# Hybrid decoder block: two operand kinds of the first output projection split into pairs early, second-half convolution outputs stored whole, T2 stored whole, one step between a fetch and its use

## The chip, the cores and the metric

One core of one Trainium2 chip runs the whole block. The metric is device time in microseconds (us); lower is better. The kernel before was timed in three runs; a profile of one further execution gives the trace that is read here. TensorE is called PE, its weight loads PEld, VectorE DVE, ScalarE ACT, GpSimd POOL, and SyncE SP; SP issues nearly all DMAs.

## The reference, cut to what matters

```python
h = rmsnorm(x, norm1_g)                                    # x: 2048 positions x 1024
p_q, p_k, p_v, p_g, p_a, c_b, c_c, c_h = split(h @ w_in)   # one input projection
o_gla = rmsnorm(gla_chunked(q, k, v, log_a), gla_norm_g) * silu(p_g)   # 4 heads x 128
o_conv = c_b * causal_depthwise_conv(c_c * c_h, conv_w)    # 512 wide, width 3
x = x + concat([o_gla, o_conv]) @ w_out                    # the output projection
h2 = rmsnorm(x, norm2_g)
x = x + (silu(h2 @ w_ffn_gate) * (h2 @ w_ffn_up)) @ w_ffn_down
return rmsnorm(x, norm_f_g)
```

Everything is float32. `gla_chunked` is gated linear attention with a state carried along the positions, so it runs in order.

## The kernel before, in words

**Layout.** Features lie on the 128 partitions and positions on the free axis, in four blocks of 512. The first *half* is blocks 0 and 1, the second half blocks 2 and 3.

**Pairs.** A float32 operand is multiplied as a pair: `split` (L206, L207) makes `hi` on ACT (a rounded copy) and `lo` on DVE (the rest). One product of two pairs is three 128x512 matmuls in a row: `wh*xh` (L503), `wh*xl` (L504) and `wl*xh` (L505), which are nearly all of PE's work.

**Units.** `unit` computes a 2x2 block of output tiles by seven products instead of eight (`PRODUCTS`: A11*B11, S1*T1, S2*T2, A12*B21, S3*T3, S4*B22, A22*T4). A, S are weight quarters and their sums, made and split inside the unit; B, T are activation operands, four tiles of 128x512 of each kind. A product takes 12 matmuls in most units, so a unit is 84. Between products an ACT copy (`copied`, L549) or a DVE addition (`plus`, L537) takes a PSUM bank's content out; the next product that accumulates into that bank waits for it. `weights_in_step` (with `after=`) makes the weights of a unit product by product, bound to the unit's own progress; `unit_weights` makes them as soon as the scheduler finds room.

**Operands from memory.** An operand kind is stored to DRAM either as a finished pair (twice the bytes, `load_pair` brings both parts) or whole (`load_undivided`), and then it is split on ACT and DVE where `due(n)` calls for it in the first unit, or at once (`load_whole`). `WHOLE` names the kinds T3, B22 and T4 that are stored whole.

**Order of the program.** (1) `opening`; (2) `in_proj(0)`, the units of the first half; (3) `in_proj(1)`, twelve units on the second half, here called second-half units 0 to 11: two for k and q, two for v, two for the gate, and twice three (cc, ch, cb) for the convolution; (4) `out_proj_in_sevens`, four units of the first half's output projection, here out-projection units 0 to 3; (5) `out_proj`, the plain output projection of the second half; (6) the feed-forward layer, both halves. Beside the units runs a list of *background* steps (`tick`, called after each product, takes steps from it; most run at every second product): `h1_ahead` makes the operands of the second half, `gate` the forget gate, `gla_half(0)` and `gla_half(1)` the attention chunks (16 in all), `mix_differences` the differences of the mixed outputs. `gla_half` fetches a chunk with 14 small DMAs, takes an exponential of the decay `ee` on ACT (L1173, L1174), multiplies (L1175, L1176), and then PE makes scores, transposes and outputs. All chunks and units take their PSUM banks from one pool of eight.

**Places that matter here.** In (3), the multiplication by c_b (L1121) finishes convolution outputs; in the second half each is split at once (eight splits, `hi<-c` on ACT and `c<-c,hi` on DVE) and stored as a pair. At the end of (3), `mix_operands` loads the operands of (4); B11 and T1 come whole and all eight of their tiles are split in one go, the kinds behind them at their `due` points. A scheduler sets the order of each engine's instructions when the program is built; `behind(marks)` and `issue_after` tell it what an instruction has to stand behind. Each engine then works its queue off in that order.

In the trace, second-half unit 0 lies at 259 to 284 us, unit 2 at 307 to 336, unit 9 at 483 to 514, unit 11 at 542 to 568; out-projection unit 0 at 568 to 603, unit 3 at 650 to 674.

Of the kernel before, what the change touches and what calls it, by code (L numbers as in the profile page):

```python
# [46 lines left out]
WHOLE = ("T3", "B22", "T4")  # L47

# [6 lines left out]
def tile_hymba_block(ctx, tc, x, xt, win, wa, wgu, wout, wffn, wdown, wdown_first, small, out):  # L55
# [54 lines left out]
    def made_ahead(name, n):  # L110
        return dram.tile([P, PB] if n in WHOLE else [P, 2, PB], F32, name=name)

# [3 lines left out]
    s_mix = [  # L116
        [dram.tile([P] + parts[b] + [PB], F32, name=f"sm{b}_{k}") for k in range(4)]
        for b in range(NB)
    ]
# [21 lines left out]
        n: [made_ahead(f"sh{n}_{k}", n) for k in range(4)] for _, n in PRODUCTS  # L141
    }
    s_h1 = {
        n: [made_ahead(f"si{n}_{k}", n) for k in range(4)] for _, n in PRODUCTS
# [129 lines left out]
    pace, ahead, hurry, steady, hasty = [0], [], [], [], []  # L274
# [232 lines left out]
    def unit(src, ops, into=None, onto=None, raw=None, between=(), rest=None, after=None, midway=None):  # L507
# [46 lines left out]
        c11 = copied("c11", oa, (0, 0))  # L554
        next(flow, None)
# [428 lines left out]
    def load_pairs(src):  # L984
        ops = no_operands()
        for _, n in PRODUCTS:
            ops[n] = [(load_undivided if n in WHOLE else load_pair)(p) for p in src[n]]
            if n in WHOLE:
                undivided[n] = ops[n]
        return ops  # L990
# [90 lines left out]
    def in_proj(half, ops, raw=None, between=(), rest=None):  # L1081
        def units():
            if half == 0:
                yield unit(win[2], ops, raw=raw, between=between, rest=rest)
            for u in range(0 if half else 3, 12):
                yield unit(win[u], ops, after=2 if half and u < 3 else None)
# [12 lines left out]
        for i0 in (0, 2):  # L1099
# [19 lines left out]
            for r, j, c, _ in next(units):  # L1119
                y = made[r, j] = cc[r, j]  # L1120
                dve.tensor_tensor(y[:], c[:], y[:], ALU.mult)  # L1121
                if half == 0:
                    store(s_mix[j][i0 + r][:], y[:])
                    if (r, 1 - j) in made:
                        t1 = tt("t1")
                        dve.tensor_tensor(t1[:], made[r, 1][:], made[r, 0][:], ALU.subtract)
                        store(s_diff["T1"][i0 + r][:], t1[:])
                    continue
                hi = tp.tile([P, PB], F32R, name="hi", tag="t")
                split(y[:], hi[:], y[:].bitcast(F32R))  # L1130
                dst = s_mix[2 * half + j][i0 + r]
                store(dst[:, 0, :], hi[:].bitcast(F32))
                store(dst[:, 1, :], y[:])


    def gla_half(half):
# [4 lines left out]
        yield  # L1141
        with tc.issue_after(tables.ins):
# [186 lines left out]

    def mix_operands():  # L1330
        src = {"B11": [y[:] for y in s_mix[0]], "B21": [s_gla[0][:, k] for k in range(4)]}
        src.update({"B22": [s_gla[1][:, k] for k in range(4)], **s_diff})
# [137 lines left out]
    def h2_ahead(ssq):  # L1470
# [8 lines left out]
        def put(n, k, h):  # L1479
            if n in WHOLE:  # L1480
# [6 lines left out]
    def load_h2():  # L1487
        ops, loads = no_operands(), raw_loads[-2]
        for _, n in PRODUCTS:
            for k in range(4):  # L1490
                with tc.issue_after(loads.ins):
                    o = (load_whole if n in WHOLE else load_pair)(s_h2p[n][k])
# [308 lines left out]
    ops = load_pairs(s_h1)  # L1801
    background.extend(
# [123 lines left out]
```

## Time and profile before

| | us |
|---|---|
| median of 3 runs (lowest, highest) | 2045.01 (2043.81, 2049.0) |
| the profiled execution's own time | 2044.2 |
| its span, first to last instruction | 2042.4 |
| PE busy in the span | 2010.8 |
| DVE busy | 1574.5 |
| ACT busy | 981.9 |

The span is 1.8 us shorter than the profiled execution's own time: what lies around it is small. In windows, the columns are window, length, then busy time and (count) of PE, PEld, DVE, ACT and POOL, the granted share of the PE clock (PEclk), the mean busy share of the 16 DMA engines, and GB/s. In a list of waits, a row is the waiting engine, its tile and line, what ended the wait, and then total us, times, longest us. In a timeline, a row is start, length, engine, line, operation, out<-in, and in brackets the idle time before it and what ended it; equal neighbours are one row with a count.

### The profile page before, as it was taken

The numbers are of one execution on the slowest core, as the hardware profiler recorded it, in microseconds if no ns is written. First come the engines' busy times: TensorE is split into PE (matmuls) and PEld (weight loads), VectorE is DVE, ScalarE is ACT, GpSimd is POOL, SyncE is SP. The second block draws the span as 40 slices with busy tenths as digits, with TensorE's granted clock in tenths as the row PEclk, the third lists the DMA queues.
The fourth block names the chain that finished last, engine by engine and source line by source line (L and its number), as shares of the span: only waits on it lengthen the run. The fifth ranks groups of instructions, "written<-read, shape, count | busy, mean of one in ns | idle before, by whom it ended". The sixth has DMA issues, their size and how long they took to land.

```text
span 2042.4 us, 27016 instructions
## 1 busy us (share of the span) xinstructions
PE 2010.8 (98%) x9251; PEld 1652.8 (81%) x9251; DVE 1574.5 (77%) x2831; ACT 981.9 (48%) x1941; POOL 10.3 (1%) x17
## 2 busy tenths in 40 slices
PE   9999999998989999999999999999999999999998
PEld 8888877787868888888888888887888888888886
DVE  7878868558887787778777688887777767778886
ACT  6664455654654344444444452334434444454345
POOL 0000000000000000000000000000000000000001
PEclk9999999999989999999999999999999999999998
DMA  7356865437687973446445576577444444486653
GB/s 263 128 202 219 285 260 176 135 122 266 194 277 246 346 269 134 170 171 219 164 159 196 192 292 242 188 283 292 157 168 170 158 147 170 175 331 221 247 216 129
DMA packets 192426, 427.78 MB, mean 209 GB/s; under 512 B 20544, under 2 KB 63776, under 8 KB 182816
## 3 DMA queue, kind: packets, MB, share of 16 engines
q1 hardware_dynamic: 191568, 425.40, 58.5%
q8 instruction: 73, 1.20, 0.2%
q10 hardware_dynamic: 720, 0.66, 0.1%
q14 instruction: 65, 0.53, 0.1%
HBM read 280.22 MB, written 145.75 MB: 209 GB/s over the span
## 4 chain that ended last, share of the span: by engine, by line
PE 94%; DVE 2%; ACT 2%; DMA 1%; issue 0%; SPq 0%; POOL 0%; POOLq 0%; DVEq 0%; ACTq 0%
PE mm L503 28%; PE mm L505 27%; PE mm L504 27%; PE mm L1394 1%; PE mm L1391 1%; PE mm L1392 1%; PE a_ps L1030 1%; PE mm L811 1%; PE mm L813 1%; PE mm L812 1%; PE o_ps L1211 1%; PE mm L1711 1%; DMA op<-sdT 1%; DVE wq L207 0%; PE o_ps L1218 0%
## 5 line engine op out<-in xcount | busy, mean ns | idle before, releaser
L503 PE MATMUL mm<-op,wq 128*128 128x512 f32 x2555 | 997.7, 393 | 9.2 <-ACT c L549 6.5
L504 PE MATMUL mm<-op,wq 128*128 128x512 f32 x2555 | 995.3, 390 | 0.0
L505 PE MATMUL mm<-op,wq 128*128 128x512 f32 x2555 | 985.9, 391 | 3.2 <-DVE wq L207 3.0
L206 ACT ACTIVATE wq<-raw 128x512 fp32r<-128x512 f32 (+2 forms) x620 | 362.1, 588 | 594.7 <-PE mm L505 500.3
L503 PEld LDWEIGHTS mm<-op,wq 128*128 128x128 f32 x2555 | 480.8, 188 | 115.9 <-ACT c L549 8.1
L505 PEld LDWEIGHTS mm<-op,wq 128*128 128x128 f32 x2555 | 480.7, 188 | 105.8 <-DVE wq L207 5.2
L504 PEld LDWEIGHTS mm<-op,wq 128*128 128x128 f32 x2555 | 481.1, 188 | 99.6 <-DVE op L207 1.5
L207 DVE TENSOR_TENSOR wq<-raw,wq 128x512 fp32r<-128x512 f32 (+2 forms) x620 | 390.9, 635 | 148.5 <-ACT wq L206 146.7
L537 DVE TENSOR_TENSOR y<-mm,y 128x512 f32<-128x512 f32 x213 | 145.6, 687 | 68.8 <-PE mm L505 67.9
L537 DVE TENSOR_TENSOR c<-mm,c 128x512 f32<-128x512 f32 x196 | 134.6, 687 | 74.3 <-PE mm L505 69.4
L549 ACT ACTIVATE c<-mm 128x512 f32<-128x512 f32 x198 | 115.3, 588 | 31.6 <-PE mm L505 28.4
L455 DVE TENSOR_TENSOR raw<-raw 128x512 f32<-128x512 f32 (+2 forms) x190 | 118.7, 631 | 2.2
L206 ACT ACTIVATE wq<-s 128x512 fp32r<-128x512 f32 (+2 forms) x100 | 58.9, 589 | 111.9 <-PE mm L505 98.5
L455 DVE TENSOR_TENSOR s<-raw 128x512 f32<-128x512 f32 (+2 forms) x95 | 60.0, 631 | 29.0 <-DMA raw<-in_wffn_dram 17.2
L207 DVE TENSOR_TENSOR op<-op 128x512 fp32r<-128x512 f32 x118 | 77.5, 682 | 3.7 <-ACT op L206 3.6
L206 ACT ACTIVATE op<-op 128x512 fp32r<-128x512 f32 x118 | 68.2, 621 | 11.4 <-DMA op<-sgla 5.2
L207 DVE TENSOR_TENSOR wq<-s,wq 128x512 fp32r<-128x512 f32 (+2 forms) x100 | 63.4, 634 | 2.1 <-ACT wq L206 1.3
L455 DVE TENSOR_TENSOR raw<-s,raw 128x512 f32<-128x512 f32 (+2 forms) x95 | 60.1, 633 | 1.4
L607 ACT ACTIVATE sg<-mm 128x512 f32<-128x512 f32 x26 | 15.5, 598 | 87.4 <-PE mm L505 87.3
L607 ACT ACTIVATE c<-c 128x512 f32<-128x512 f32 x78 | 48.9, 629 | 13.1 <-DVE c L537 10.5
L1392 PE MATMUL mm<-op,wq 128*128 128x512 f32 x128 | 50.2, 392 | 0.0
L1391 PE MATMUL mm<-op,wq 128*128 128x512 f32 x128 | 49.8, 389 | 0.0
(234 smaller groups left out, 1546.3 us busy)
## 6 DMA issues: line engine op xcount, KB each, us to landing
raw<-in_wffn_dram SPq DMA_DIRECT2D x44, 1024.0 KB, 6.2
sa_B<-so SPq DMA_DIRECT2D x47, 512.0 KB, 3.6
op<-sa_B SPq DMA_DIRECT2D x47, 512.0 KB, 6.5
raw<-in_win_dram SPq DMA_DIRECT2D x22, 1024.0 KB, 5.7
sa_T<-so SPq DMA_DIRECT2D x44, 512.0 KB, 4.4
op<-sa_T SPq DMA_DIRECT2D x44, 512.0 KB, 6.9
raw<-in_wdown_dram SPq DMA_DIRECT2D x24, 768.0 KB, 5.5
sx<-y SPq DMA_DIRECT2D x48, 256.0 KB, 4.1
```

What stands on the lines that cost most here:

```text
L206: last_hi[:] = [act.activation(hi, src, AF.Copy)]
L207: last_lo[:] = [dve.tensor_tensor(lo, src, hi.bitcast(F32), ALU.subtract)]
L455: dve.tensor_tensor(*args)
L503: pe.matmul(o[:], wh, xh, start=first and k == 0, stop=False, skip_group_check=True)
L504: pe.matmul(o[:], wh, xl, start=False, stop=False, skip_group_check=True)
L505: return pe.matmul(o[:], wl, xh, start=False, stop=k == n - 1, skip_group_check=True)
L537: last_plus[:] = [dve.tensor_tensor(t[:], o[:], t[:], ALU.add)]
L549: last_out[:] = [act.activation(t[:], o[:], AF.Copy)]
L607: last_silu[:] = [act.activation(s[:], c[:], AF.Silu)]
L811: pe.matmul(acc[:], wq[:, 0, c], p[:, 0, :], start=first, stop=False)
L1391: pe.matmul(o[e, j][:], wh, m[:, 0, :], start=n == 0, stop=False)
L1392: pe.matmul(o[e, j][:], wh, m[:, 1, :], start=False, stop=False)
```

## The change

- A list `MOSTLY` adds **T2** to the kinds stored whole, for the second half's input operands (`s_h1`) and the feed-forward operands made ahead (`s_h2p`). T2's splits move: for the input projection to a new `due("T2")` after the first product of second-half unit 0, for the feed-forward layer to its loading.
- **Early pairs.** A new generator `early_pairs` loads the eight tiles of B11 and T1 of the first output projection one by one, splits each and stores it as a pair (`s_pair`); `tick` takes one of its steps at every fourth product when nothing more urgent is due, and `mix_operands` runs what is left. Then `mix_operands` loads B11 and T1 with `load_pair`.
- **Convolution outputs** of the second half are stored whole. `build_mix` loads them with `load_whole`, which splits them there, marked to stand behind the fourth last `plus`.
- **Second-half unit 2** has its weights made by `unit_weights` instead of in step (`u < 2` for `u < 3`).
- `gla_half(1)` gets one more step between its first fetch and the first exponential.

```diff
+MOSTLY = ("T2", "T3", "B22", "T4")
...
-    s_mix = [
-        [dram.tile([P] + parts[b] + [PB], F32, name=f"sm{b}_{k}") for k in range(4)]
-        for b in range(NB)
-    ]
+    s_mix = scratch("sm", 4)
+    s_pair = {
+        n: [dram.tile([P, 2, PB], F32, name=f"sp{n}_{k}") for k in range(4)] for n in ("B11", "T1")
+    }
...
         elif hasty and pace[0] % 4 == 3:
             step()
+        elif pairs and pace[0] % 4 == 1:
+            next(pairs[0], None)
         elif ahead and pace[0] % 4 == 1:
             next(ahead[0], None)
...
         c11 = copied("c11", oa, (0, 0))
+        due("T2")
         next(flow, None)
...
     def h1_ahead():
         def put(n, k, h):
-            if n in WHOLE:
+            if n in MOSTLY:
                 store(s_h1[n][k][:], h[:])
...
-                yield unit(win[u], ops, after=2 if half and u < 3 else None)
+                yield unit(win[u], ops, after=2 if half and u < 2 else None)
...
-                if half == 0:
-                    store(s_mix[j][i0 + r][:], y[:])
...
-                hi = tp.tile([P, PB], F32R, name="hi", tag="t")
-                split(y[:], hi[:], y[:].bitcast(F32R))
-                dst = s_mix[2 * half + j][i0 + r]
-                store(dst[:, 0, :], hi[:].bitcast(F32))
-                store(dst[:, 1, :], y[:])
+                store(s_mix[2 * half + j][i0 + r][:], y[:])
...
         fetched = gla_fetch(*chunks[0])
         yield
+        if half:
+            yield
         with tc.issue_after(tables.ins):
             cur = gla_scaled(*fetched)
...
+    def early_pairs():
+        for n, sources in (("B11", s_mix[0]), ("T1", s_diff["T1"])):
+            for k in range(4):
+                h = tt("h")
+                load(h[:], sources[k][:])
+                yield
+                hi = tp.tile([P, PB], F32R, name="hi", tag="t")
+                with behind(last_out + last_plus):
+                    split(h[:], hi[:], h[:].bitcast(F32R))
+                for e, p in enumerate((hi, h)):
+                    store(s_pair[n][k][:, e, :], p[:].bitcast(F32))
+                yield
+
     def mix_operands():
+        for _ in pairs.pop():
+            pass
...
-            ops[n] = [(load_pair if n == "T2" else load_undivided)(p) for p in src[n]]
-            if n in ("B11", "T1"):
-                with behind(last_out):
-                    for o in ops[n]:
-                        split(o[:, 1, :].bitcast(F32), o[:, 0, :], o[:, 1, :])
-            elif n != "T2":
+            paired = n in ("B11", "T1", "T2")
+            ops[n] = [(load_pair if paired else load_undivided)(p) for p in src[n]]
+            if not paired:
                 undivided[n] = ops[n]
...
     def build_mix():
         def pair(b, k):
-            return load_pair(s_gla[b][:, k] if k < HEADS else s_mix[b][k - HEADS])
+            if k < HEADS:
+                return load_pair(s_gla[b][:, k])
+            with behind([all_plus[-4]]):
+                return load_whole(s_mix[b][k - HEADS])
...
     ops = load_pairs(s_h1)
+    pairs.append(early_pairs())
```

The built programs show three places. Numbers in names are buffers and differ between the two programs; line numbers of the changed program are its own (its L207 and L208 are `split`, L552 is `copied`, L1171 and L1172 the two exponentials, L1125 the multiplication by c_b, L1076 and L1080 the gate's scan and difference, L458 the weight sums).

The first is ACT's queue in second-half unit 9, around the first exponential of `gla_half(1)`; `hi<-c` are convolution splits, `c11<-mm` and `c22<-mm` the copies that release the unit's first two banks. Before:

```order
L206 ACTIVATE wq_5026<-raw_5015 128x512
L206 ACTIVATE wq_5029<-raw_5015 128x512
L206 ACTIVATE hi_4953<-h_4894 128x512
L206 ACTIVATE wq_5032<-raw_5015 128x512
L206 ACTIVATE hi_4997<-c22_4505 128x512
L1173 ACTIVATE ee_4973<-ee_4973 128x256
L1174 ACTIVATE ee_4973<-ee_4973 128x256
L206 ACTIVATE hi_5003<-c12_4519 128x512
L206 ACTIVATE hi_5009<-c11_4618 128x512
L549 ACTIVATE c11_5059<-mm_5042 128x512
L549 ACTIVATE c22_5094<-mm_5061 128x512
```

The same place of the changed program:

```order
L552 ACTIVATE c11_5077<-mm_5064 128x512
L207 ACTIVATE wq_5048<-raw_5037 128x512
L207 ACTIVATE wq_5051<-raw_5037 128x512
L207 ACTIVATE hi_4991<-h_4932 128x512
L207 ACTIVATE wq_5054<-raw_5037 128x512
L552 ACTIVATE c22_5096<-mm_5079 128x512
L1171 ACTIVATE ee_5011<-ee_5011 128x256
L1172 ACTIVATE ee_5011<-ee_5011 128x256
L552 ACTIVATE c12_5130<-mm_5064 128x512
```

The two copies now stand ahead of the exponential, the third copy c12 behind it, and the convolution splits are gone from here.

The second is DVE's queue at the head of out-projection unit 0; `op<-op` are operand splits, `c11_5312<-mm_5624` (before) and `c11_5290<-mm_5631` (changed) the last multiplication by c_b, which reads a PSUM bank. Before, ten rows of it, behind eight splits of B11 and T1 that stand further up:

```order
L207 TENSOR_TENSOR op_5932<-op_5932 128x512
L1121 TENSOR_TENSOR c12_5168<-c12_5732,c12_5168 128x512
L207 TENSOR_TENSOR op_5934<-op_5934 128x512
L207 TENSOR_TENSOR osb_5676<-osb_5676,gt_5407 128x512
L207 TENSOR_TENSOR op_5936<-op_5936 128x512
L207 TENSOR_TENSOR op_5938<-op_5938 128x512
L1246 TENSOR_SCALAR hsq_5835<-hsq_5835 128x4
L207 TENSOR_TENSOR c22_5094<-c22_5094,hi_5863 128x512
L1237 TENSOR_SCALAR state0_109<-state0_109,dn_3205,kvs_5829 128x128
L1121 TENSOR_TENSOR c11_5312<-mm_5624,c11_5312 128x512
```

Of the changed program:

```order
L540 TENSOR_TENSOR c12_5748<-mm_5670,c12_5748 128x512
L1260 TENSOR_SCALAR osb_5741<-ot_5840,sml_99,gt_5451 128x512
L208 TENSOR_TENSOR wq_5932<-raw_5920,wq_5932 128x512
L1125 TENSOR_TENSOR c12_5130<-c12_5748,c12_5130 128x512
L208 TENSOR_TENSOR op_5886<-op_5886 128x512
L208 TENSOR_TENSOR op_5888<-op_5888 128x512
L1125 TENSOR_TENSOR c11_5290<-mm_5631,c11_5290 128x512
```

Two operand splits stand ahead of that multiplication where there were fourteen with the eight of B11 and T1, and no convolution split where there were two.

The third is DVE's queue in second-half unit 2, where `g1<-ones,g2` are the gate's scans and `wq` the weight splits. Before:

```order
L1072 TENSOR_SCALAR g1_3209<-ones_92,g2_3210 128x128 x4
L455 TENSOR_TENSOR s1_3598<-raw_3599 128x512
L1072 TENSOR_SCALAR g1_3240<-ones_92,g2_3241 128x128 x4
L207 TENSOR_TENSOR wq_3323<-raw_3311,wq_3323 128x512
L207 TENSOR_TENSOR wq_3326<-raw_3311,wq_3326 128x512
L207 TENSOR_TENSOR wq_3344<-raw_3311,wq_3344 128x512
```

Of the changed program:

```order
L208 TENSOR_TENSOR wq_3326<-raw_3315,wq_3326 128x512
L1073 TENSOR_SCALAR g2_3213<-g2_3213,g1_3212 128x512
L1080 TENSOR_TENSOR g2_3174<-g1_3173 128x512
L1073 TENSOR_SCALAR g2_3244<-g2_3244,g1_3243 128x512
L1174 TENSOR_SCALAR kq_3273<-kq_3273,ee_3274 128x256
L458 TENSOR_TENSOR s1_3608<-raw_3609 128x512
L208 TENSOR_TENSOR wq_3329<-raw_3315,wq_3329 128x512
L1082 TENSOR_TENSOR dn_3134<-em_3133,el_3135 128x4
L1076 TENSOR_SCALAR g1_3212<-ones_92,g2_3213 128x128 x4
L208 TENSOR_TENSOR wq_3332<-raw_3315,wq_3332 128x512
```

The weight splits for the unit's third product (`wq_3323` before, `wq_3326` now) have moved ahead of the last eight scans.

Each engine has as many instructions in both programs except SP, which issues 12 DMAs more: 8 loads and 16 stores of the early pairs, less 4 stores of T2 and 8 of convolution outputs.

More of the change, by code (lines that the diff above doesn't have):

```diff
@@ L108, in scratch, with made_ahead @@
         ]
-    def made_ahead(name, n):
-        return dram.tile([P, PB] if n in WHOLE else [P, 2, PB], F32, name=name)
+    def made_ahead(name, n, whole=WHOLE):
+        return dram.tile([P, PB] if n in whole else [P, 2, PB], F32, name=name)
     s_kq, s_d, s_v, s_g = scratch("sk", 4), scratch("sd", 2), scratch("sv", 4), scratch("sg", 4)
@@ L140, in tile_hymba_block @@
     s_h2p = {
[L141 removed]
+        n: [made_ahead(f"sh{n}_{k}", n, MOSTLY) for k in range(4)] for _, n in PRODUCTS
     }
     s_h1 = {
[L144 removed]
+        n: [made_ahead(f"si{n}_{k}", n, MOSTLY) for k in range(4)] for _, n in PRODUCTS
     }
@@ L273, in tile_hymba_block @@
     background = []
-    pace, ahead, hurry, steady, hasty = [0], [], [], [], []
+    pace, ahead, hurry, steady, hasty, pairs = [0], [], [], [], [], []
     def step():
@@ L986, in load_pairs @@
         for _, n in PRODUCTS:
-            ops[n] = [(load_undivided if n in WHOLE else load_pair)(p) for p in src[n]]
-            if n in WHOLE:
+            ops[n] = [(load_undivided if n in MOSTLY else load_pair)(p) for p in src[n]]
+            if n in MOSTLY:
                 undivided[n] = ops[n]
```

17 lines of the change are left out of this document (8 added, 9 removed).

## Prediction

> **What bounds the kernel now.** I read the page first: span, busy time, granted clock.
>
> ```profile
> span 2042.4 us, 27016 instructions
> PE 2010.8 (98%) x9251; PEld 1652.8 (81%) x9251; DVE 1574.5 (77%) x2831; ACT 981.9 (48%) x1941; POOL 10.3 (1%) x17
> PEclk9999999999989999999999999999999999999998
> ```
>
> PE is busy but for 31.6 us, and the change leaves its matmuls as they are (as many instructions on PE in both programs). So the time can only come from PE's idle time and from stretches in which its clock was cut. The list of PE's waits between 280 and 640 us, second, says where half of that idle time lies.
>
> ```profile
> PE mm L503 <- ACT c L549: 5.4, 2, 4.9
> PE v_ps L1195 <- ACT ee L1196: 4.2, 1, 4.2
> PE kt_ps L1192 <- DVE c L1121: 3.1, 1, 3.1
> PE mm L505 <- DVE wq L207: 3.0, 2, 2.6
> PE mm L503 <- DVE y L537: 0.9, 1, 0.9
> ```
>
> Third, windows of 20 us give the clock that goes with them.
>
> ```profile
> 300.00:320.00 20.00, 17.43 (x81) 13.68 (x80) 17.24 (x40) 12.63 (x29) 0.00 (x0) 0.97 0.54 178
> 320.00:340.00 20.00, 20.00 (x116) 16.15 (x116) 16.05 (x37) 10.91 (x37) 0.00 (x0) 0.95 0.63 192
> 480.00:500.00 20.00, 15.14 (x68) 11.93 (x67) 17.42 (x31) 8.46 (x16) 0.00 (x0) 0.91 0.91 308
> 560.00:580.00 20.00, 14.99 (x88) 11.88 (x86) 16.86 (x32) 12.86 (x31) 0.00 (x0) 0.95 0.82 272
> 580.00:600.00 20.00, 16.77 (x76) 13.54 (x78) 16.74 (x35) 8.45 (x18) 0.00 (x0) 0.79 0.91 334
> ```
>
> Three places, then; everywhere else between 320 and 560 us the clock is 1.00 or nearly so. What each is worth now:
>
> - **Place C, second-half unit 2** (about 315 us): one wait of 2.6 for a weight split, and a clock short by (0.03 + 0.05) x 20 = 1.6 us. Together 4.2.
> - **Place B, second-half unit 9** (about 490): one wait of 4.9 for the copy c, and (1 - 0.91) x 20 = 1.8 of clock. Together 6.7.
> - **Place A, head of out-projection unit 0** (574 to 592): 3.1 + 4.2 + 0.9 = 8.2 of waits. The clock is short by (0.05 + 0.21) x 20 = 5.2 us, which at half clock means 10.4 us of it; 5.1 of those (the 4.2 and the 0.9) are taken as idle, so 5.3 worked slowly and lost half: 2.7. Together 10.9.
>
> In sum 21.8 us, 1.1% of the time.
>
> **What causes each place, and what the change does to it.** B first, in ACT's timeline, with SP's row of the load and PE's row of the wait:
>
> ```profile
> 486.97 0.63 ACT L206 ACTIVATE hi<-c 128x512 fp32r<-128x512 f32 x1 [0.22 <-DVE c L1121]
> 490.77 0.42 ACT L1173 ACTIVATE ee<-ee 128x256 f32<-128x256 f32 x1 [3.16 <-DMA ee<-sd]
> 491.54 1.13 ACT L206 ACTIVATE hi<-c 128x512 fp32r<-128x512 f32 x2
> 492.58 1.06 ACT L549 ACTIVATE c<-mm 128x512 f32<-128x512 f32 x2
> 488.18 0.99 SPq L160 DMA_DIRECT2D ee<-sd  x2
> 493.21 0.80 PE L503 MATMUL mm<-op,wq 128*128 128x512 f32 x1 [4.86 <-ACT c L549]
> ```
>
> ACT stands 3.16 us before the exponential, whose load SP issued only at 488.2; behind it in the queue are two convolution splits (1.1) and then the copies that PE needs. In the changed program both copies stand ahead of the exponential and the splits are gone. But the load is hardly sooner in SP's queue, and the third copy, c12, stands behind the exponential. PE runs S2*T2 next (12 matmuls), then needs c12. If the exponential again starts at 490.8, c12 is out at about 490.8 + 0.8 (two exponentials) + 0.6 = 492.2, while S2*T2, starting at 488.2, ends at 490.9 (12 matmuls at 0.227 us). So a wait of about 1.4 stays; I take 1.5. B gives 6.7 - 1.5 = **5.2**; bounds 1.8 (the wait only changes its name) to 6.7.
>
> A is a queue that is too full, on DVE. Five windows, one per unit from second-half unit 10 on, and two groups of DVE in the two middle ones (542 to 603), with one timeline row for the pitch:
>
> ```profile
> 517.00:542.00 25.00, 25.00 (x144) 20.22 (x141) 19.31 (x47) 14.71 (x44) 0.00 (x0) 1.00 0.51 145
> 542.00:568.00 26.00, 26.00 (x155) 21.22 (x154) 23.96 (x47) 16.22 (x40) 0.00 (x0) 1.00 0.74 241
> 568.00:603.00 35.00, 26.75 (x128) 21.19 (x127) 29.98 (x57) 20.84 (x50) 0.00 (x0) 0.85 0.88 312
> 603.00:628.00 25.00, 25.00 (x139) 19.85 (x138) 22.30 (x53) 13.90 (x40) 0.00 (x0) 1.00 0.75 234
> 628.00:650.00 22.00, 22.00 (x113) 18.21 (x112) 16.21 (x30) 10.09 (x24) 0.00 (x0) 1.00 0.53 167
> L207 DVE TENSOR_TENSOR op<-op 128x512 fp32r<-128x512 f32 x24 | 15.5, 682 | 2.1 <-ACT op L206 2.1
> L207 DVE TENSOR_TENSOR c<-c,hi 128x512 fp32r<-128x512 f32 x4 | 2.7, 680 | 0.0
> 587.58 1.88 DVE L207 TENSOR_TENSOR op<-op 128x512 fp32r<-128x512 f32 x3
> ```
>
> Three splits take 1.88, so one more costs 0.60. In 542 to 603 DVE is busy for 23.96 + 29.98 = 53.9 us; PE alone would need 61 - 10.9 = 50.1. DVE is the bound there: the last multiplication by c_b waits in its queue behind the operand splits, holds a PSUM bank, and kt_ps waits for the bank. The change takes 8 operand splits of B11 and T1 and 4 convolution splits out: 12 x 0.60 = 7.2; one early-pair split comes in. DVE then needs 47.3 for PE's 50.1. Ahead of that multiplication the queue is shorter by 12 operand splits and 2 convolution splits, 14 x 0.60 = 8.4 us, against 8.2 us of waits. The margin is thin (94%), and the twelve splits of T3, B22 and T4 now stand between PE's products, each just in time. I leave 2.0 of waiting there: A gives **8.9**; bounds 2.9 (three quarters stay) to 10.9.
>
> C is an order, in DVE's timeline:
>
> ```profile
> 309.94 0.67 DVE L207 TENSOR_TENSOR wq<-s,wq 128x512 fp32r<-128x512 f32 x1
> 313.87 1.36 DVE L1072 TENSOR_TENSOR_SCAN g<-ones,g 128x128 f32<-128x128 f32 x4
> 315.74 1.36 DVE L1072 TENSOR_TENSOR_SCAN g<-ones,g 128x128 f32<-128x128 f32 x4
> 317.02 1.87 DVE L207 TENSOR_TENSOR wq<-raw,wq 128x512 fp32r<-128x512 f32 x3
> ```
>
> The lo of the third product's weights was made at 317.0, behind 8 scans. Now one 128x512 operation stands between it and the split of 309.94, so it is done near 309.94 + 3 x 0.60 = 311.7, some 5 us before PE wants it. The fifth product's weights come after four scans, about when PE gets there; I leave 0.4. C gives **3.8**; bounds 1.6 to 4.2.
>
> **What the change adds.** Four terms, each hidden in part.
>
> ```profile
> 266.00 0.69 DVE L207 TENSOR_TENSOR wq<-raw,wq 128x512 fp32r<-128x512 f32 x1 [1.16 <-ACT wq L206]
> 270.29 0.69 DVE L537 TENSOR_TENSOR c<-mm,c 128x512 f32<-128x512 f32 x1 [3.60 <-PE mm L505]
> 528.90 0.33 SPq L160 DMA_DIRECT2D raw<-in_wout_dram  x1
> raw<-in_wout_dram SPq DMA_DIRECT2D x8, 1024.0 KB, 7.1
> 648.00:674.00 26.00, 26.00 (x117) 21.49 (x116) 15.18 (x24) 7.90 (x13) 0.00 (x0) 1.00 0.98 371
> 1390.07 0.63 ACT L206 ACTIVATE wq<-s 128x512 fp32r<-128x512 f32 x1 [4.80 <-DVE s L481]
> ```
>
> - *T2 in second-half unit 0:* four splits, 4 x 0.60 = 2.4 on DVE, between the first and the third product, where DVE idled 1.16 + 3.60. Hidden, but four ACT splits now stand ahead of one copy: **0.7** (0 to 2.4).
> - *Head of second-half unit 11:* the first output weights (1 MB, 7.1 us from issue to landing) were issued at 528.9, long before their first sum on DVE. Now SP issues them behind a chunk's 14 small loads and the last early-pair load, and ten DVE operations (about 6 us) later DVE's queue has that sum, with the operation that frees a PSUM bank behind it. The wait is 7.1 - 6 = 1.1, more if SP is late: **1.5** (0 to 5).
> - *Out-projection unit 3:* eight convolution splits, 4.8 on DVE and about 4.2 on ACT, in a window where DVE is busy 15.2 and ACT 7.9 of 26. They wait for loads into buffers that become free product by product, with weight splits behind them: **0.8** (0 to 4.8). The loads are half as large, where the DMA engines were 98% busy.
> - *T2 before the feed-forward layer's second half:* four splits beside an ACT that idles 4.8 us: **0.3** (0 to 2.4).
>
> The rest lies beside other work: early pairs' seven other splits go one by one into units where PE is the bound, and T2's splits leave background steps on which PE did not wait, which gives nothing. SP's 12 more issues take 0.3 to 0.5 us each and are spread over some 250 us. B11 and T1 come in as 512 KB instead of 256 (2 MB more) in a stretch with DMA shares of 0.74 to 0.88; that is in the second term's range. A chunk's later last store leaves out_proj's attention loads about 5 us later, with four convolution heads' matmuls (48 x 0.227 = 10.9 us) ahead of their use.
>
> **Sum.** -5.2 - 8.9 - 3.8 + 0.7 + 1.5 + 0.8 + 0.3 = -14.6 on the profiled execution's 2044.2: **2029.6** us. The median of the runs is 0.8 higher, so this is 0.7 to 0.8% faster by either.
>
> A wait of 2.6 us at C was enough here to cut the clock (0.97 and 0.95 in the two windows). The Trainium skill, "TensorE: Matmul & The Clock Gate", section "What's actually happening", says that the clock halves after at least one idle window of about 3.4 us, which by itself would leave C's 1.6 us of clock unexplained. By that rule C would hold only 2.6 us and the sum would be 1.6 us smaller; the rows decide.
>
> **Rivals.**
>
> - *All three places close and nothing is added:* 2044.2 - 21.8 = **2022.4**. For it speaks the slack of each added term; against it the exponential that still waits in ACT's queue, and DVE at 94% of PE in A.
> - *The waits change their owner:* B keeps its wait through c12 (gain 1.8), A's backlog meets the late weights and three quarters stay (2.9), C gives 3.8, and the added terms cost 3.3: **2039.0**. For it: the load of `ee` stands where it stood, so this part of the change doesn't do what it says, a load a step sooner.
> - *DVE becomes the bound of all five windows and the kernel slower:* in 517 to 650 DVE is busy 111.8 of 133 us (84%). The change takes out 7.2 and puts in two early-pair splits, 1.2: 105.8. If just-in-time splits, each of which waits for ACT and that for a DMA, leave DVE working 70% of the time, the stretch takes 105.8 / 0.70 = 151, 18 more than now; with B and C gained (9.0) and the three added terms outside (1.8) that is 2044.2 + 18 - 9.0 + 1.8 = **2055**. It turns slower by over 0.3% (6.1 us) below 72%. Against it: when its queue was fullest, 568 to 603, DVE was 86% busy.
>
> **Chances.** Forecast 0.60, clean 0.20, waits moved 0.13, slower 0.07. About 0.3%, 6 us, is what a measurement can tell from no change. Forecast and clean are faster by more: 0.80; waits moved ends 0.25% below, within it: 0.13; slower 0.07. The low end is the clean case with 2 us for small waits (0.4 to 1.0 each) that may go as well: 2020; the high end takes in the moved waits with some room: 2041.
>
> **What would show it.** Right: in the changed profile PE's list has no wait for L1121's successor and none for a weight split in unit 2; c12 in unit 9 costs 1 to 2 us; PEclk shows no loss near 315 and 575. DVE's sum in the five windows falls by about 6 us, and the DMA wait of the weight sum at the head of unit 11 is 1 to 2. Wrong: a wait of 3 us or more for `raw<-in_wout_dram` or for a convolution tile's load in ACT's queue, which would cut the clock anew; or a gap at unit 0's third product.

## The result, and the profile after

| | before | changed |
|---|---|---|
| median of 22 runs (lowest, highest), us | 2045.0 (2042.89, 2051.01) | 2048.16 (2045.06, 2056.5) |
| the profiled execution's own time, span | 2044.2, 2042.4 | 2048.33, 2046.6 |
| ratio, 95% interval | | 1.0019, [1.0011, 1.0026] |

The change made the kernel 0.2% slower, where 0.7% faster was forecast. The page's first lines are nearly those of before:

```profile
span 2046.6 us, 27017 instructions
PE 2010.6 (98%) x9251; PEld 1652.4 (81%) x9251; DVE 1573.0 (77%) x2831; ACT 979.5 (48%) x1941; POOL 10.3 (1%) x17
PEclk9999999999999999999999999999999999999999
```

PE's idle time is 2046.6 - 2010.6 = 36.0 us, 4.4 more than before. To see where, I took each unit's *loss* in both traces: how far each PE instruction's start lies behind the one before it, beyond the pitch that it has at full speed (0.227 us for a 128x512 matmul, 0.11 to 0.12 for the chunks' smaller ones), summed over the unit. That puts waits and clock into one number and leaves out the chunks' own matmuls, which the extra step moves from unit to unit (2.6 us of them leave unit 9). A wait ahead of a unit's first matmul counts to the unit before it.

| place | forecast | change of loss |
|---|---|---|
| all before second-half unit 0 | 0 | +1.1 |
| unit 0 (T2 split there) | +0.7 | +1.0 |
| unit 2 (place C) | -3.8 | -2.6 |
| unit 5 | 0 | **+3.1** |
| unit 8 | 0 | -0.5 |
| unit 9 (place B) | -5.2 | -3.8 |
| units 10 and 11 | +1.5 | **+4.3** |
| out-projection units 0, 1, 2 (place A) | -8.9 | **-0.7** |
| unit 3 and the plain projection | +0.8 | +2.1 |
| feed-forward layer | +0.3 | +1.1 |
| sum | -14.6 | +5.1 |

(The last matmul starts 4.5 us later than before; the other 0.6 comes of pricing the chunks' small matmuls so roughly. The first row lies outside the five places. In the experiments below unit 0 starts 0.1 to 0.8 later than before where T2 is whole, and 0 to 0.4 sooner where it is not, so part of that row may be T2's; this was not tested.) So B and C came to about 70% of their forecast, A did not come, and the gain was lost at places forecast at little or nothing. PE's waits between 280 and 700 us in the changed kernel, longest in total first:

```profile
PE mm L506 <- ACT c L552: 5.6, 4, 2.0
PE ot L1259 <- DVE osb L1250: 3.6, 2, 2.5
PE mm L506 <- issue: 2.9, 1, 2.9
PE mm L506 <- ACT op L207: 2.7, 1, 2.7
PE mm L506 <- DVE y L540: 2.4, 2, 1.6
PE o_ps L1209 <- DVE scores L1187: 1.8, 1, 1.8
```

The two waits of place A (kt_ps for c, v_ps for ee) and C's wait for a weight split are gone, and no wait is longer than 2.9 (for that one the profile names nothing that ended it). But there are eleven where there were eight. The five windows of the prediction, 517 to 650 us:

```profile
517.00:542.00 25.00, 25.00 (x157) 20.23 (x156) 19.80 (x43) 16.08 (x49) 0.00 (x0) 1.00 0.46 132
542.00:568.00 26.00, 22.33 (x122) 17.60 (x121) 19.40 (x45) 10.78 (x29) 0.00 (x0) 1.00 0.86 288
568.00:603.00 35.00, 28.64 (x136) 22.47 (x135) 25.18 (x50) 18.46 (x43) 0.00 (x0) 0.90 0.95 335
603.00:628.00 25.00, 25.00 (x143) 20.12 (x143) 22.86 (x48) 13.39 (x36) 0.00 (x0) 1.00 0.74 228
628.00:650.00 22.00, 22.00 (x119) 17.93 (x116) 16.89 (x35) 10.70 (x31) 0.00 (x0) 1.00 0.58 195
```

DVE's busy time from 542 to 603 fell from 53.9 to 44.6, more than the 47.3 forecast, and yet PE's fell too, from 52.8 to 51.0. So DVE no longer bounds that stretch, and something else holds PE up. ACT's own waits from 540 to 610 point to it, first before, then after:

```profile
ACT op L206 <- DMA op<-sgla: 5.2, 2, 3.4
```

```profile
ACT op L207 <- DMA op<-sgla: 12.9, 3, 6.7
ACT ee L1171 <- DMA ee<-sd: 4.0, 2, 2.7
```

ACT, which works in order, stands 12.9 us before operand splits whose tiles are not loaded. The loads are issued late, as SP's queue shows. The rows are the loads of one attention chunk (`kq<-sk`, the third last) and of the first output projection's operands, before and after:

```profile
531.87 2.14 SPq L160 DMA_DIRECT2D kq<-sk  x4
543.44 2.40 SPq L160 DMA_DIRECT2D op<-sm  x4
564.62 1.80 SPq L160 DMA_DIRECT2D op<-sgla  x4
```

```profile
541.29 2.39 SPq L161 DMA_DIRECT2D op<-spB  x4
548.64 3.11 SPq L161 DMA_DIRECT2D kq<-sk  x4
565.45 1.04 SPq L161 DMA_DIRECT2D op<-sgla  x2
578.67 0.91 SPq L161 DMA_DIRECT2D op<-sgla  x2
```

The chunk that was fetched at 531.9, ahead of all operand loads, is fetched at 548.6 behind the first of them, and two loads of B21 go out at 578.7 instead of 565. The DMA engines are busier as well (0.86 and 0.95 in the windows from 542 and 568, where the prediction's rows have 0.74 and 0.88). B went as forecast in kind, with c12 behind the exponential in ACT's queue:

```profile
490.43 0.60 ACT L552 ACTIVATE c<-mm 128x512 f32<-128x512 f32 x1 [1.63 <-PE mm L508]
493.70 0.42 ACT L1171 ACTIVATE ee<-ee 128x256 f32<-128x256 f32 x1 [2.67 <-DMA ee<-sd]
494.15 0.42 ACT L1172 ACTIVATE ee<-ee 128x256 f32<-128x256 f32 x1
494.48 0.58 ACT L552 ACTIVATE c<-mm 128x512 f32<-128x512 f32 x1
```

### The profile page after: what moved, and what is told of

It reads as the page before. It is cut to its first block, busy times and chain, and to the rows that moved or that the text cites. A ratio compares the mean times of both kernels' runs of the same rounds, so it can differ in the third digit from the quotient of the medians.

```text
span 2046.6 us, 27017 instructions
## 1 busy us (share of the span) xinstructions
PE 2010.6 (98%) x9251; PEld 1652.4 (81%) x9251; DVE 1573.0 (77%) x2831; ACT 979.5 (48%) x1941; POOL 10.3 (1%) x17
## 4 chain that ended last, share of the span: by engine, by line
PE 91%; DVE 4%; DMA 2%; ACT 1%; issue 1%; SPq 1%; POOL 0%; POOLq 0%; DVEq 0%; ACTq 0%
PE mm L506 27%; PE mm L508 26%; PE mm L507 26%; PE mm L1407 1%; PE mm L1404 1%; PE mm L1405 1%; PE mm L815 1%; PE a_ps L1034 1%; PE mm L817 1%; PE mm L816 1%; DVE wq L208 1%; DVE op L208 1%; PE mm L1724 1%; SPq L161 1%; PE o_ps L1209 1%
## 5 line engine op out<-in xcount | busy, mean ns | idle before, releaser
L207 ACT ACTIVATE wq<-raw 128x512 fp32r<-128x512 f32 (+2 forms) x620 | 362.0, 588 | 589.7 <-PE mm L508 492.5
L208 DVE TENSOR_TENSOR wq<-raw,wq 128x512 fp32r<-128x512 f32 (+2 forms) x620 | 391.3, 636 | 147.7 <-ACT wq L207 145.7
L552 ACT ACTIVATE c<-mm 128x512 f32<-128x512 f32 x198 | 115.3, 588 | 32.1 <-PE mm L508 28.6
L458 DVE TENSOR_TENSOR raw<-raw 128x512 f32<-128x512 f32 (+2 forms) x192 | 120.2, 632 | 2.2
L207 ACT ACTIVATE wq<-s 128x512 fp32r<-128x512 f32 (+2 forms) x100 | 58.9, 589 | 111.9 <-PE mm L508 100.2
L208 DVE TENSOR_TENSOR op<-op 128x512 fp32r<-128x512 f32 x126 | 82.6, 684 | 14.2 <-ACT op L207 14.2
L458 DVE TENSOR_TENSOR s<-raw 128x512 f32<-128x512 f32 (+2 forms) x96 | 60.7, 632 | 35.6 <-DMA raw<-in_wffn_dram 26.3
L207 ACT ACTIVATE op<-op 128x512 fp32r<-128x512 f32 x126 | 72.6, 620 | 25.0 <-DMA op<-sgla 12.9
L208 DVE TENSOR_TENSOR wq<-s,wq 128x512 fp32r<-128x512 f32 (+2 forms) x100 | 63.5, 635 | 2.4 <-ACT wq L207 1.6
L458 DVE TENSOR_TENSOR raw<-s,raw 128x512 f32<-128x512 f32 (+2 forms) x96 | 60.8, 634 | 1.4
```

What stands on the lines that cost most here:

```text
L207: last_hi[:] = [act.activation(hi, src, AF.Copy)]
L208: last_lo[:] = [dve.tensor_tensor(lo, src, hi.bitcast(F32), ALU.subtract)]
L458: dve.tensor_tensor(*args)
L552: last_out[:] = [act.activation(t[:], o[:], AF.Copy)]
```

## The experiments

The parts of the change are called *conv* (convolution outputs whole), *unit 2* (its weights early), *T2* (T2 whole), *pairs* (early pairs) and *step* (the extra step in `gla_half(1)`). Two theories stood at first. "Pairs": the early pairs cost more in SP's queue than they save on DVE. "Step": the extra step has pushed every later chunk onto the output projection's loads.

| run | parts | median | ratio to before, 95% |
|---|---|---|---|
| c3_conv_only | conv | 2037.71 | 0.997 [0.9959, 0.9981] |
| d1_conv_and_unit2 | conv, unit 2 | 2034.66 | 0.9954 [0.994, 0.9968] |
| e2_no_pairs_no_step | conv, unit 2, T2 | 2039.41 | 0.9974 [0.9963, 0.9984] |
| c1_no_pairs | conv, unit 2, T2, step | 2049.34 | 1.0024 [1.0016, 1.0033] |
| c2_no_step | conv, unit 2, T2, pairs | 2048.03 | 1.0022 [1.0013, 1.0031] |
| (the change) | all five | 2048.16 | 1.0019 [1.0011, 1.0026] |
| c4_pairs_only | pairs | 2053.44 | 1.0046 [1.0034, 1.0058] |
| d2_step_only | step | 2058.86 | 1.0085 [1.0072, 1.0097] |

**One part left out.** c1 undoes the early pairs, c2 the extra step:

```diff
-    pairs.append(early_pairs())
...
-            paired = n in ("B11", "T1", "T2")
+            ops[n] = [(load_pair if n == "T2" else load_undivided)(p) for p in src[n]]
+            if n in ("B11", "T1"):
+                with behind(last_out):
+                    for o in ops[n]:
+                        split(o[:, 1, :].bitcast(F32), o[:, 0, :], o[:, 1, :])
```

> The changed kernel without early pairs: B11 and T1 are loaded whole and split at the head of out-projection unit 0, as before; the other four parts stay. Theory 'pairs': the early pairs' stores wait in SP's queue for their splits and hold up the loads of the next chunk. Then the 2.1 us wait behind the exponential at second-half unit 5 (399 us) goes and its clock loss of 1.8 with it (3.5 us in all), and the waits at unit 11 shrink; total 3.5 to 8 us below the changed kernel, so 2040 to 2044. Theory 'step': the extra background step has put each later chunk's loads one step later, onto the loads of the first output projection; then units 10, 11 and out-projection unit 0 keep their losses, only unit 5 gains, and the eight splits come back to DVE: 2045 to 2050.

```diff
         fetched = gla_fetch(*chunks[0])
         yield
-        if half:
-            yield
```

> The changed kernel without the extra step before the first exponential of the second attention half; the other four parts stay. Theory 'step': the chunk loads stand again where they stood before the change, ahead of the pair loads for the first output projection; units 10 and 11 lose nothing (4.6 us back) and out-projection unit 0 gains most of what was forecast (about 6 us more), so 2037 to 2041. Theory 'pairs': units 10 and 11 still lose, since the stores of the pairs stand in SP's queue; 2046 to 2049, and unit 9 waits longer, the exponential's load being a step less ahead.

Without pairs, unit 5's loss rose by 0.2 instead of 3.1: so the pairs cause it. But unit 11 lost 15.2 more than before, of which out-projection unit 0 gave 9.5 back. Without the step, units 10 and 11 lost nothing more, and in out-projection unit 0, up to its last matmul, PE lost 8.7 less than before: place A's gain is there. But the head of unit 1 then costs some 12 us, a wait of 9.4 and the clock behind it, so units 0 and 1 together lost 3.3 more. Both theories were half right, and c2's total lies in the range of "pairs" although units 10 and 11 did not do what that theory says: each part has its own place where it costs. PE's longest wait without pairs, and DVE's queue that ends it:

```profile
PE ot L1259 <- DVE osb L1250: 14.3, 3, 11.6
```

```profile
569.26 2.49 DVE L208 TENSOR_TENSOR op<-op 128x512 fp32r<-128x512 f32 x4
571.67 0.69 DVE L458 TENSOR_TENSOR raw<-raw 128x512 f32<-128x512 f32 x1
572.27 0.16 DVE L221 SCALAR_TENSOR_TENSOR hsq<-hl,hy 128x4 f32<-128x4 f32 x1
572.34 2.49 DVE L208 TENSOR_TENSOR op<-op 128x512 fp32r<-128x512 f32 x4
574.75 0.75 DVE L1250 TENSOR_TENSOR osb<-o_ps,hsq 128x256 f32<-128x256 f32 x2
```

The chunk, a step late, has its `osb` behind the output projection's operand splits, on a DVE that first stands 4.6 us for an exponential and then works from 549.9 to 575 with hardly a pause. That is the collision that the step makes. The longest wait without the step is another one, at the head of out-projection unit 1. PE's row, then two of ACT's waits from 560 to 610:

```profile
PE mm L506 <- ACT wq L207: 9.4, 1, 9.4
```

```profile
ACT wq L207 <- DMA raw<-in_wout_dram: 7.1, 1, 7.1
ACT op L207 <- DMA op<-sgla: 6.2, 2, 5.4
```

**One part alone.** c3 has only the hunks of `s_mix`, of the c_b multiplication and of `build_mix`; c4 only `early_pairs` with its caller; d2 only the step.

> The kernel before with only the second half's convolution outputs stored whole. Both theories: unit 9's two copies stand ahead of the exponential and the 4.9 us wait there falls to about 2 (5 to 6 us of time with the clock). If what was gained there is given back by chunks that then come too late for units 10 and 11, whatever else is changed, units 10 and 11 lose 4 us here too, 2043 to 2046; if that loss comes from the extra step or the pairs, they lose nothing, 2037 to 2040. Out-projection unit 3 to the plain projection adds 1 to 2 in either case.

> The kernel before with only the early pairs. Theory 'pairs': 3 us lost at second-half unit 5, the wait at unit 9 (4.9) as before, and out-projection unit 0 improves by less than 3, its operands coming late behind SP's queue; 2044 to 2049. Theory 'step': 3 us lost at unit 5 likewise, but out-projection unit 0 improves by 6 to 9 us, since eight splits leave DVE's queue there and the loads are not pushed back; 2038 to 2042.

> The kernel before with only the extra step before the first exponential of the second attention half. If the step does what it is named for, the load of the exponential lands in time, unit 9's wait of 4.9 falls below 2 and the time to 2039 to 2042. If it only shifts every later chunk onto the first output projection's loads and operand splits, unit 9 waits as before, units 10 and 11 lose 4 to 16 us, part of it taken out of out-projection unit 0 again: 2047 to 2056.

Convolution outputs alone gain: unit 9 -2.8, unit 8 -0.9, out-projection unit 0 -3.2, the plain projection +1.1; units 10 and 11 lose nothing. So what B gains is not given back by itself. The pairs alone end above the range that either theory gave: unit 5 +3.1 and out-projection units 0 and 1 +2.1 and +2.6, with PE waiting 9.9 for weights at the end of unit 0 (without this wait unit 0 lost 7.9 less than before). The step alone is the worst of all, above its range too. Unit 9 waits as before (5.9 where 4.9 was): the exponential's load goes out no sooner in the unit (6.1 us after its start, 5.4 before), and ACT stands 4.2 us for it with the copies behind. Then unit 11 loses 21.3 more and out-projection unit 0 8.9 less. ACT's row, then PE's two longest waits:

```profile
489.88 0.42 ACT L1180 ACTIVATE ee<-ee 128x256 f32<-128x256 f32 x1 [4.19 <-DMA ee<-sd]
PE ot L1268 <- DVE osb L1259: 19.4, 3, 16.5
PE mm L509 <- ACT c L555: 7.6, 3, 5.9
```

**Two and three parts.** d1 adds unit 2 to the convolution outputs, e2 adds T2 to both:

```diff
-                yield unit(win[u], ops, after=2 if half and u < 3 else None)
+                yield unit(win[u], ops, after=2 if half and u < 2 else None)
```

> The kernel before with convolution outputs stored whole and second-half unit 2's weights made early; no pairs, no extra step, T2 as before. If the two gains add, unit 2 shortens by 2.6 to 4.4 us as it did in the runs that had this edit, and the rest is as with convolution outputs alone: 2033 to 2035.5. If what unit 2 gains is given back by chunks that then come too late, 2037 to 2039.

```diff
-WHOLE = ("T3", "B22", "T4")
+MOSTLY = ("T2", "T3", "B22", "T4")
...
         c11 = copied("c11", oa, (0, 0))
+        due("T2")
```

> The changed kernel without early pairs and without the extra step: convolution outputs whole, unit 2's weights early, T2 whole. Against 2034.7 without T2 whole this gives the price of T2: 0.5 us in second-half unit 0 and 1 to 2.4 before the feed-forward layer's second half, 2036 to 2038. If T2's price is larger where the pairs are present only (unit 0 lost 2.1 there in two runs), it is 2035 to 2036.

d1 gained 4.8 in unit 2 and kept it: 0.46% faster than before, the fastest version found. T2 costs more than forecast: ratio 0.9974 against 0.9954, some 4 us, though the two intervals just overlap. In e2's trace unit 0 loses 2.6 more (a 1.7 us wait for an operand split and a clock of 0.92 from 268 to 290 us) and the feed-forward layer takes 3.8 longer, with this wait at 1385 us, where before PE waited for no weight split:

```profile
PE mm L506 <- ACT wq L207: 2.7, 1, 2.7
```

That last part isn't T2's alone: d1 (1.6) and c4 (3.7), without T2, lose time at that place too, on an operand's split. And e2's traced execution, 2044.71, was the slowest of its eight, so a usual one may lose less. Both waits of place A stay in e2, which has no pairs:

```profile
PE kt_ps L1188 <- DVE c L1125: 4.5, 1, 4.5
PE v_ps L1191 <- ACT ee L1192: 2.7, 1, 2.7
```

**Late weights.** d3 is c2 with the next output weights asked for ahead of the operand loads:

```diff
+        raws = [out_weights(0), out_weights(2)]
+        ops = ops()
...
-            raw = raw_weights(wout[d0 // 2]).rearrange("p a (b e c) -> p (a b) e c", e=2, c=P)
+            raw = raws.pop(0)
+            if 0 < d0 and d0 + 2 < KD:
+                raws.append(out_weights(d0 + 2))
...
-    ssq = out_proj_in_sevens(residual(0), mix_operands())
+    ssq = out_proj_in_sevens(residual(0), mix_operands)
```

> The changed kernel without the extra step, and with the output weights of out-projection unit 1 asked for ahead of the operand loads, so that the load stands in SP's queue near the end of second-half unit 11 rather than at the end of out-projection unit 0. Theory 'late weights': the 9.4 us wait for a weight split at the head of out-projection unit 1 goes, with 2.5 us of clock; against 2048.0 without this edit, 2036 to 2040. Rival: the operands' own loads then come late by as much (1 MB moves ahead of them), and out-projection unit 0 takes over the wait: 2044 to 2049.

SP issues unit 1's weights at these times before, in c2 (with the next unit's), and in d3:

```profile
575.59 0.42 SPq L160 DMA_DIRECT2D raw<-in_wout_dram  x1
```

```profile
596.25 1.12 SPq L161 DMA_DIRECT2D raw<-in_wout_dram  x2
```

```profile
562.61 0.39 SPq L161 DMA_DIRECT2D raw<-in_wout_dram  x1
```

The 9.4 us wait is gone; the median is 2041.99 and the ratio 0.9999 [0.999, 1.0007], where c2 had 1.0022. It missed its range by 2: out-projection unit 0 gains 6.1 on before, but units 1 and 2 lose 2.6 and 1.6. So the pairs had displaced the weights: in c2 the scheduler put that load 21 us later in SP's queue, behind all the operand loads and a chunk's fourteen. In the changed kernel it goes out at 592.9 and with the pairs alone (c4) at 602.0; in the five kernels without pairs, between 571 and 581.

**The stores.** d4 and e1 are c2 with the pairs' stores a step later, or issued by POOL; f1 leaves one store out.

```diff
                     split(h[:], hi[:], h[:].bitcast(F32R))
+                yield
                 for e, p in enumerate((hi, h)):
```

> The changed kernel without the extra step, and with the early pairs stored one of their steps after the split. Theory: at second-half unit 5 SP stood with the store of a pair's lo at the head of its queue until DVE had made it, and the chunk's loads stood behind; with the store a step later unit 5 is as long as before (3.1 us back), 2044 to 2046 if nothing else moves. Rival: it is the pairs' splits and transfers, not the place of the stores; unit 5 keeps its 3.1 us, 2047 to 2049.

```diff
-                    store(s_pair[n][k][:, e, :], p[:].bitcast(F32))
+                    nc.gpsimd.dma_start(s_pair[n][k][:, e, :], p[:].bitcast(F32))
```

> The changed kernel without the extra step, and with the early pairs' stores issued by POOL instead of SP; nothing else is changed. Theory: at second-half unit 5 SP stood behind a pair's store of lo until DVE had made it, and the next chunk's loads, the exponential and the copies behind it came late by as much; with the store out of SP's queue the exponential's load is issued some 0.5 to 1 us sooner, and unit 5 is again as long as before (3.1 us back); the late weights at out-projection unit 1 stay: 2043 to 2047. Rival: the splits and transfers of the pairs themselves make unit 5 long; 3 us stay there, 2047 to 2050.

```diff
                 for e, p in enumerate((hi, h)):
-                    store(s_pair[n][k][:, e, :], p[:].bitcast(F32))
+                    if (n, k, e) != ("B11", 3, 1):
+                        store(s_pair[n][k][:, e, :], p[:].bitcast(F32))
...
+        src["B11"] = src["B11"][:3] + src["B11"][2:3]
```

> The changed kernel without the extra step, and without one of the pairs' sixteen stores: the second half (lo) of B11's fourth tile is not stored (out-projection units read the third tile's pair in its place, so part of the output is computed from the wrong tile); its load and its split stay. This store is the one that goes out at the head of second-half unit 5, 256 KB just ahead of the next chunk's loads. If it is this store, through SP's queue and the transfers that its write delays, unit 5 is again as long as before (3 us back) and the load of the exponential lands in about 2 us as before, not 3.6. If it is the split on ACT and DVE, unit 5 keeps its 3 us. The total tells little, 2043 to 2048 in either case.

d4 (2050.22, 1.0035 [1.0022, 1.0048]) tells nothing on unit 5: the scheduler kept a store at the same place ahead of the chunk's loads. It shows something else: with three steps a pair, the pairs were not ready, and PE waited up to 8.3 us for `op<-spT` loads at out-projection unit 0. e1 (2046.59, 1.0009 [1.0001, 1.0017]) kept 3.0 of unit 5's 3.1, so that its total lies in the theory's range without the theory's reason. f1 (2046.63, 1.0015 [1.0005, 1.0024]) kept 2.1: PE waited 1.6 and 0.6 there where it waited 1.9, and the clock was not cut (1.00 from 396 to 425, against 0.94). So my theory falls: the store, in SP's queue or as a transfer, is at most a third of it, and PE's waits didn't get shorter without it. What the traces have in common with the pairs: SP issued only one of the chunk's `kq` loads, or none, before it came to stand at a gate store (two, before the change), so that the exponential's loads go out 0.5 to 1.0 later in the unit and land later, in 2.8 to 3.9 us (median of the two) where 2.0 was usual. SP's and ACT's rows, before and in the changed kernel:

```profile
385.51 0.92 SPq L160 DMA_DIRECT2D kq<-sk  x2
393.92 0.85 SPq L160 DMA_DIRECT2D ee<-sd  x2
396.34 1.28 ACT L1173 ACT_TABLE_LOAD   x1 [2.08 <-DMA ee<-sd]
```

```profile
390.90 0.32 SPq L164 DMA_DIRECT2D spB<-h  x1
392.38 1.88 SPq L161 DMA_DIRECT2D kq<-sk  x4
394.36 0.86 SPq L161 DMA_DIRECT2D ee<-sd  x2
398.33 1.28 ACT L1171 ACT_TABLE_LOAD   x1 [4.58 <-DMA ee<-sd]
```

That the pairs cost unit 5 its 3 us is shown (every kernel with them loses 2.1 to 3.4 there, every one without at most 0.2); by which of the issue's delay and the slower landing is only argued.

**A best try.** e3 has conv and unit 2, and the pairs with both remedies (POOL's stores and d3's weights).

> Early pairs with their stores on POOL and with the next output weights asked for ahead of the operand loads, convolution outputs whole, unit 2's weights early; no T2, no extra step. If the early pairs are worth what was forecast once their two prices (the stores in SP's queue, the late weights) are taken away, out-projection unit 0 gains 3 to 4 us more than without pairs: 2030 to 2033. If the operand loads still come late behind the chunks' loads in SP's queue, the pairs gain nothing: 2034 to 2038.

It came to 2041.37, 0.9982 [0.9973, 0.9991], slower than without the pairs at all (d1) and above both of its ranges. Out-projection unit 0 lost 8.2 less than before, nearly the 8.9 forecast for A. But units 1 and 2, unit 3 and the plain projection gave 10.6 back. PE's three longest waits between 240 and 720 us:

```profile
PE v_ps L1190 <- DVE y L540: 4.6, 1, 4.6
PE mm L506 <- ACT c L552: 4.1, 3, 2.2
PE mm L1412 <- DVE wq L208: 2.3, 1, 2.3
```

At the end of the next unit PE waits for a bank that DVE has to empty (4.6 us at 617), and in the plain projection for a weight split. The gain is there, and it isn't kept.

## Why the prediction was wrong, step by step

- **The step that failed is place A's -8.9**, worked out from DVE's queue alone ("Ahead of that multiplication the queue is shorter by 12 operand splits and 2 convolution splits"). That part was right: DVE's busy time fell to 44.6 us, and the waits for c and ee vanished. With pairs and without the step PE lost 8.7 (c2) and 7.9 (c4) less in unit 0 itself, and without pairs (e2) both waits stay. But the sum took the loads as given; the pairs' 2 MB more were put into the range of another term. The pairs put eight 512 KB loads in SP's queue where eight of 256 KB had been, and with them the scheduler moved what stood behind: unit 1's weights by 17 to 26 us, which without the step is the 9.4 us wait at unit 1's head, and in the changed kernel two of B21's four loads by 13. Asking for the weights sooner took that wait away, but of the gain at unit 0 (6.1 in d3, 8.2 in e3) units 1 and 2 and what follows gave part or all back. So A came to -0.7 for -8.9. SP's queue wasn't fuller for it: from 542 to 603 SP spends 33.8 us issuing, before 33.9. Its order changed, and loads landed later as well (B21's first two in 7.4 and 7.5 us, before in 3.2 and 5.2). How much is the order's and how much the transfers', no run separates.
- **The early pairs were costed at almost nothing** ("The rest lies beside other work"). They cost 3.1 at unit 5, and, added to conv, unit 2 and T2, 0.48% in all (c2 against e2). How they do it at unit 5 stays open.
- **The extra step was costed only by the output weights' load**, +1.5 at unit 11. That load hardly moved (528.57, before 528.90). What moved was every chunk behind the step, by one background step, into the output projection's loads: +4.3 in units 10 and 11 beside the pairs; 0.50% in all without them (c1 against e2), and 16.0 us alone. The wait came where the prediction looked for one, for another reason.
- **B** (-5.2): the order of the copies was read rightly, c12 costs 2.0 where 1.5 was taken, and a chunk's transposes then wait 1.1 more; -3.8 came. It comes from the convolution outputs, not from the extra step: with these alone unit 9 loses 2.8 less, with the step alone 2.4 more.
- **C** (-3.8): -2.6 beside the rest, since a wait of 1.8 for a chunk's scores behind the scans took part of it (the row of `o_ps` above); -4.8 without pairs and T2 (d1).
- **T2**: unit 0 +1.0 for +0.7; before the feed-forward layer's second half +1.1 for +0.3. Where the clock is cut as well it is 2.6 at unit 0.
- **Convolution splits in the plain projection** (+0.8): +1.1 alone, +2.1 in the changed kernel.
- **The rivals.** "The waits change their owner" was right in kind and 9 us short, and its reason that the step brings the load of `ee` no sooner is what d2 shows. Its late weights were put at unit 11; they came at out-projection unit 1, once the step was away. "DVE becomes the bound" was wrong in its bound, since DVE's sum in the five windows fell from 111.8 to 104.1; but its splits that wait for ACT, and ACT for a DMA, are what the 12.9 us of ACT show. The stretch lost 3.6 more, not 18.
- **The range's upper end**, 2041, came from "waits moved" with some room. What the pairs and the step cost meets place A in the same 60 us, on SP's queue, for which no sum was made.
- **The signs.** Most of those named for "right" came: no wait behind the last multiplication by c_b, none for a weight split in unit 2, c12 at 2.0, DVE's sum down by 7.7; only the clock behind 575 us was still cut (0.90 from 568 to 603). They tested the three places and not what came to stand there instead. A small slip: place A held some 11.2 us and not 10.9, since its 0.9 us wait at 592 lies behind the cut of the clock (578.0 to 588.2).

## What to carry to other kernels

Where work leaves a full engine, ask which loads its replacement needs and write out the issuing queue there, load by load, as was done here for ACT and DVE: a moved load costs through what is queued behind it. A step added to a background generator moves everything that the generator does afterwards, so its price lies at the busiest later place, not where it was put. And parts of a change that meet in one stretch are tried one at a time: two of the five here gave 0.46%, and the other three took it back.

## What the runs showed of the hardware

The same wait may or may not cut PE's clock. At the fifth product of second-half unit 0 PE waits about 2.0 us in all kernels with T2 (1.7 for an operand split, 0.3 for its lo; before, 1.0). In four of the eight profiled kernels with T2 the clock was cut there, in four not. The record of the granted clock in the traces says why. Between 60 and 1990 us all cuts of a trace start a whole number of steps of 3.413 us apart and last 3.4, 6.8 or more such steps: in the kernel before they start at 318.6, 492.7 and 578.0, which is 51 and 25 steps. Windows on this grid, first c2, then the changed kernel:

```profile
270.20:273.60 3.40, 1.37 (x5) 0.59 (x5) 1.56 (x3) 2.71 (x6) 0.00 (x0) 1.00 1.05 405
273.60:277.00 3.40, 3.40 (x9) 2.61 (x9) 3.40 (x7) 3.40 (x7) 0.00 (x0) 0.51 1.08 422
```

```profile
268.90:272.30 3.40, 2.46 (x11) 1.69 (x9) 1.07 (x2) 0.90 (x2) 0.00 (x0) 1.00 1.05 404
272.30:275.70 3.40, 2.30 (x9) 1.68 (x10) 3.15 (x6) 3.40 (x8) 0.00 (x0) 1.00 1.06 407
```

In c2 the whole wait lies in one window. PE is idle for 3.40 - 1.37 = 2.03 us of it, and the next window runs at half the clock, which loses 0.49 x 3.4 = 1.7 us. In the changed kernel the border of two windows falls into the wait; PE is idle for 0.94 and 1.10 of them, and nothing is cut. So it is in all 14 traces, with 7848 such windows at full clock: none in which PE was idle for less than 1.6 us was followed by a cut, and every one with more than 1.9 was; in between both occur. The Trainium skill, "TensorE: Matmul & The Clock Gate", section "What's actually happening", has a free-running window of about 3.4 us, whose phase at the kernel's start varies from run to run; the grid and the length of the cuts agree with that, though 1.9 us without work, shorter than the window, were enough.

So a kernel with many waits of 1 to 3 us may run unevenly. The changed kernel's 22 runs spread over 11.4 us and those of the kernel before over 8.1; whether the clock is the reason was not tested apart.
